# A planner that reckons a longer landing for small adding loads, with the output's and gate's steps placed anew

## The chip, the cores and the metric

One core of one Trainium2 chip runs the whole program once per launch. The metric is the device time of one execution in microseconds (us). The time of the kernel before is the median of three runs, 981.69 us (978.53 to 984.54).

## The reference: what is computed

One layer of a decoder trunk is applied to 1024 prompt positions and to 8 sample positions (one new position of each of 8 sequences), with a model width of 1024. All data are fp32.

```python
xn = rmsnorm(x, pre_g)
u, v, z_a, x_b, z_b, g_a, g_b = split(xn @ w_in)          # seven parts of 1024 columns
y_a = gelu(u) * (tril(w_s) layernorm(gelu(v)) + b_s) * silu(z_a)   # mixed inside chunks of 128
y_b = pooled_linear(x_b) * silu(z_b)                      # trailing windows of 2, 4, 8, 16
m = sigmoid(g_a) * (y_a @ w_pa) + sigmoid(g_b) * (y_b @ w_pb)
h = x + rmsnorm(m @ w_out, post_g)
y = h + rmsnorm(sigmoid(rmsnorm(h, ple_in_g) @ w_pg) * (p @ w_ple), ple_out_g)
```

The outputs are y of the prompt and of the sample, and small states (normalised v rows, pooling rows).

## The kernel before, in words

**Products.** Each large product is cut into 2x2 quarters and done in seven block products instead of eight (functions strassen and strassen_within), and each fp32 factor is split into a high and a low float32r part, so that one block product is 12 matmuls (k = 4 slices, three terms) of 512 columns, or 24 of 260. The blocks have the names of their right-hand factor: B11, T2, T3, T1, B21, B22, T4. In the last two stages the tokens stand on the left: the stage of the output (m @ w_out; tiles acct, left factors mw, right factors woB and woT) and the stage of the gate (h @ w_pg; left factors hw, right factors wgB and wgT). Each has four pairs of token tiles (pair 0 to 3, of 2 x 128 tokens), seven block products a pair. The lists oflow and gflow hold these 28 + 28 steps in order: steps 0 to 27 are the output's, 28 to 55 the gate's. Three PSUM tiles named acct go round; a product that opens a tile waits until the tile's last reader has let go of it.

**Sample rows.** The 8 sample rows go beside these, without the seven-block scheme: sample_steps loads two rows tiles of 128 x 1024 of the weight (worow, wgrow) at one step and runs 8 matmuls of 8 x 512 (tile sps) two steps later, four times. OS and GS (line 36) are the steps at which this begins in the two stages. After the last of them, out_sample adds the partial rows up (sodd, hs).

**From the output to the gate.** For each token tile and for the sample, out_finish scales the row by its norm, adds x with an adding load issued by GpSimd (`nc.gpsimd.dma_start(out=h, in_=x_of(t), accum_op=ALU.add)`) and stores h; gate_norm takes the sum of squares of the finished h on ScalarE (junk<-h, for the sample hn<-hs) and its root on GpSimd; gate_input loads h back in 32-row blocks (hblocks, four DMAs) which VectorE turns (STREAM_TRANSPOSE) into the tile big. For the sample the turning is done by TensorE (tile psst). TURNS (line 35) has for each pair the steps after which its out_finish, gate_norm and gate_input are recorded; for the sample they are the steps OS + 10, OS + 12 and OS + 15 of oflow.

**The planner.** All of this is recorded first (all instructions bear line 369, the line that plays them). Planner.take, lines 213 to 245, gives each operation a reckoned length; a DMA gets `moved` (MB, doubled for an adding load) and `lands`, the time to land on top of its bytes. Planner.wanted goes back from the clock of TensorE's recorded order and sets when each operation is due (`late`), and Planner.order then plays all five engines forward: an operation may start no sooner than its due time less a lead (LEAD, or LOAD for a load into a fresh slot), the one due soonest goes first, and slots are handed out. The order in which each engine's instructions stand, and the slot of each tile, come from this. On the chip no reckoned time is left: an instruction runs as soon as those ahead of it in its engine's queue are through and what it waits for is done. SyncE (SP) issues nearly all DMAs in one queue, where a DMA that waits for its slot holds up all behind it.

Of the kernel before, what the change touches and what calls it, by code (L numbers as in the profile page):

```python
# [31 lines left out]
PUSH = {'norm': -5.0, 'half': 0.0, 'cut': 0.0, 'e': -4.0, 'we': -4.0, 'vw': -5.0, 'p': -1.0}  # L32
WARM = 8
HASTE = 8.0
TURNS = ((7, 8, 11), (14, 14, 18), (21, 26, 28), (30, 33, 35))
OS, GS = 5, 12
WINDOWS = (2, 4, 8, 16)
PLE = 256
SLOTS = 46
# [55 lines left out]
class Planner:  # L95
# [5 lines left out]

    SEEN = {"tensor": 0.25, "vector": 0.15, "scalar": 0.20, "gpsimd": 0.20}
    TABLES = {AF.Gelu_apprx_tanh: 1, AF.Sigmoid: 2, AF.Silu: 3}
    LOAD, LEAD, PATIENCE, RATE, SPARE = 14.98, 14.0, 55.8, 0.36, 3
    SPARED = 1.0

    def __init__(self, nc, slots, queues):
# [98 lines left out]
    def take(self, engine, method, args, kwargs):  # L206
        given = [*(("out" if i == 0 else "", a) for i, a in enumerate(args)), *kwargs.items()]
        writes = [a for k, a in given if k in ("out", "accum_out") and a is not None]
        reads = [a for k, a in given if k not in ("out", "accum_out") and hasattr(a, "tensor")]
        if kwargs.get("accum_op") is not None:  # L210
            reads += writes
        name = writes[0].tensor.name
        if engine == "tensor" and self.open is not None and self.open[0] == name:
            op = self.open[1]
        else:
            op = Op(engine, len(self.ops), self.clock, self.fixed)
            op.patience, op.push = self.patience, self.push
            self.ops.append(op)
        self.open = (name, op) if engine == "tensor" else None
        op.calls.append((method, args, kwargs))  # L220
        op.spent.append(op.busy)
        if method == "dma_start":
            run = min(self.run(a) for a in (writes[0], reads[0]))
            op.busy, op.moved = 1.0 if engine == "gpsimd" else 0.45, writes[0].size() * 4e-6 * (1 + 0.2 / run)
            op.lands = 2.0
            if kwargs.get("accum_op") is not None:
                op.moved, op.lands = 2 * op.moved, 3.5
        else:
            took = self.duration(engine, method, writes[0], reads, kwargs)
            op.busy += took  # L230
            if engine == "tensor" and not self.fixed:
                self.clock += took
            if engine == "scalar":
                op.table = self.TABLES.get(kwargs["func"], 0)
        for ap in reads:
            self.touch(op, ap, False)
        for ap in writes:
            self.touch(op, ap, True)
# [133 lines left out]
@with_exitstack  # L372
def tile_hybrid_step(ctx, tc, *args):
    hybrid_step(ctx, tc, *args)


def hybrid_step(
# [116 lines left out]
    class Operand:  # L494
# [37 lines left out]
        def at(self, what, k):  # L532
            return [part[:, k % 2, :] for part in self.parts[what, k // 2]]
# [653 lines left out]
    def stored(key, src, width, free=None):  # L1187
        return Stored(key, src, kept[key + "low"], kept[key + "high"], width, free)
# [194 lines left out]
    flat, c = big.rearrange("p b t -> p (b t)"), [T + 4 * w for w in (0, HALF, HALF + WIDE, HALF + 2 * WIDE)]  # L1383
# [20 lines left out]
    c = vsteps[0]  # L1404
# [55 lines left out]
    WITHIN = ("B11", "T2", "T3", "T1", "B21", "B22", "T4")  # L1460

    def turn_over(op, loads, cuts, parts=PARTS):
        for what, l, c in zip(parts, loads, cuts):
            at(l, lambda what=what: op.load(what))
            at(c, lambda what=what: op.cut(what))

    p, l, c = gbsteps[2], gbsteps[3], pasteps[0]
    turn_over(yaop, l, [*l[1:], c[0]])
    p, l, c = pasteps[2], pasteps[3], pbsteps[0]
# [97 lines left out]
    def hasty(do, ts):  # L1567
        plan.patience = HASTE
        for t in ts:
            do(t)  # L1570
        plan.patience = plan.PATIENCE
# [61 lines left out]
    def embed_gate_sample(ps):  # L1633
# [3 lines left out]
        for j in range(2):  # L1637
# [7 lines left out]
    woop, wgop = stored("wo", w_out, HALF), stored("wg", kept["wg"], HALF)  # L1645
    outsteps = [strassen_within(Turned(i, "m"), woop, Out(i)) if i else
                strassen(Turned(i, "m"), woop, Out(i), Tokens, FIRST) for i in range(NPAIR)]
# [8 lines left out]
    l, c = pbsteps[3], outsteps[0]  # L1656
    turn_over(woop, l, [*l[2:], c[0], c[1]], ("B11", "T3", "T2", "B21", "T4", "T1", "B22"))
    l, c = outsteps[3], gatesteps[0]
    turn_over(wgop, [*outsteps[2][4:], *l], [*l[2:], c[0], c[1]], WITHIN)

    def gain_row(key, src):
        gains[key] = row_broadcast(src, key)
# [11 lines left out]
    for i in range(NPAIR):  # L1674
        ts = [2 * i + 1, 2 * i]
        for do, s in zip((out_finish, gate_norm, gate_input), TURNS[i]):
            at((oflow + gflow)[s], lambda do=do, ts=ts: hasty(do, ts))
# [198 lines left out]
```

## Time and profile before

| | before |
|---|---|
| median of three runs | 981.69 us (978.53 to 984.54) |
| profiled execution, own time | 979.92 us |
| its span, first to last instruction | 978.2 us |
| TensorE (PE) busy | 965.4 us, 99% |
| VectorE (DVE) busy | 805.7 us, 82% |
| ScalarE (ACT) busy | 495.5 us, 51% |
| GpSimd (POOL) busy | 72.8 us, 7% |
| mean granted TensorE clock | 0.997 |

In the profile, PE is the row of matmuls, PEld that of weight loads, DVE, ACT and POOL are the three other compute engines, SPq the DMA issues of SyncE. A row of the timeline has the start and length in us, the engine, the line, the operation, the tile written and the tiles read, shapes, the count, and in brackets how long the engine sat idle before it and what ended that. Matmuls overlap, so each is shown longer (0.39 us) than the 0.23 us from one start to the next.

### The profile page before, as it was taken

How to read it: one execution, taken by the hardware profiler on the slowest of the kernel's cores; microseconds unless marked ns; L12 is line 12 of the kernel's file. 1: busy time of each engine (PE TensorE's matmuls, PEld its weight loads, DVE VectorE, ACT ScalarE, POOL GpSimd, SP SyncE). 2: the span in 40 equal slices, each digit the busy share in tenths (PEclk: the TensorE clock that was granted, in tenths of full speed). 3: DMA queues.
4: the chain of work that ended last, by engine and by line, in shares of the span. 5: the costliest groups of instructions: out<-in, count | busy, mean ns of one | idle time of the engine just before them, and what ended most of it. 6: DMA issues, size and time to landing. Idle time of an engine off the chain costs nothing. (4 is left out here: it accounts for less than half of the span.)

```text
span 978.2 us, 15914 instructions
## 1 busy us (share of the span) xinstructions
PE 965.4 (99%) x6048; PEld 858.1 (88%) x6048; DVE 805.7 (82%) x1251; ACT 495.5 (51%) x847; POOL 72.8 (7%) x117
## 2 busy tenths in 40 slices
PE   9999999999999999999999999999999999999996
PEld 7889999999999998999999999999999997778775
DVE  7798568978879789887777897698699899779987
ACT  7674346767434544242423343463363273688655
POOL 2200000000000000000010100000000001323212
PEclk9999999999999999999999999999999999999998
DMA  9464654423457787541222266692592385698996
GB/s 347 148 151 88 152 135 148 162 95 116 171 213 275 257 281 238 188 153 54 87 76 93 75 218 244 222 376 91 170 370 87 120 306 177 160 300 296 222 326 209
DMA packets 128505, 185.81 MB, mean 190 GB/s; under 512 B 42150, under 2 KB 85198, under 8 KB 128421
## 3 DMA queue, kind: packets, MB, share of 16 engines
q1 hardware_dynamic: 126093, 176.91, 54.4%
q0 software_dynamic: 2048, 7.37, 4.2%
q8 instruction: 47, 0.77, 0.3%
q10 hardware_dynamic: 288, 0.52, 0.2%
q14 instruction: 29, 0.24, 0.1%
HBM read 129.27 MB, written 55.96 MB: 189 GB/s over the span
## 5 line engine op out<-in xcount | busy, mean ns | idle before, releaser
L369 DVE TENSOR_TENSOR u<-acc,u 128x520 f32<-128x520 f32 (+1 forms) x90 | 62.5, 695 | 29.8 <-PE acc L369 29.8
L369 POOL TENSOR_TENSOR rstd<-ms,mhalf 128x1 f32<-128x1 f32 (+1 forms) x37 | 30.1, 840 | 448.7 <-DVE ms L369 448.0
L369 ACT ACTIVATE u<-acc 128x512 f32<-128x512 f32 x39 | 23.2, 596 | 35.0 <-PE acc L369 32.5
L369 ACT ACTIVATE zbw<-zbs 128x512 fp32r<-128x512 f32 x16 | 10.0, 629 | 31.6 <-DVE zbs L369 25.8
L369 DVE TENSOR_TENSOR big<-big 128x1024 f32<-128x1024 f32 (+4 forms) x20 | 24.7, 1262 | 0.1
L369 POOL COPY big<-xb 128x1 f32<-128x1 f32 x8 | 3.5, 443 | 260.9 <-ACT xb L369 218.0
L369 ACT ACTIVATE big<-mix 128x256 f32<-128x256 f32 x32 | 11.9, 382 | 20.6 <-PE mix L369 19.7
L369 ACT ACTIVATE paw<-pas 128x512 fp32r<-128x512 f32 x16 | 10.1, 630 | 24.0 <-DVE pas L369 20.0
L369 ACT ACTIVATE pbw<-pbs 128x512 fp32r<-128x512 f32 x16 | 10.1, 630 | 22.3 <-DVE pbs L369 17.0
L369 PE MATMUL accm<-qh,wpoolw 128*128 128x260 f32 (+1 forms) x96 | 21.0, 320 | 0.0
L369 DVE TENSOR_TENSOR zbw<-zbs,zbw 128x512 fp32r<-128x512 f32 x16 | 10.9, 689 | 12.0 <-ACT zbw L369 11.9
L369 ACT ACTIVATE gbw<-gbs 128x512 fp32r<-128x512 f32 x16 | 10.1, 630 | 20.9 <-DVE gbs L369 11.7
L369 ACT ACT_TABLE_LOAD x11 | 14.1, 1283 | 7.4 <-PE acc L369 3.6
L369 ACT ACTIVATE junk<-h 128x512 bf16<-128x512 f32 x25 | 15.7, 627 | 3.5 <-DVE h L369 3.0
L369 DVE SCALAR_TENSOR_TENSOR zb<-accm,gvec,zb 128x512 f32<-128x512 f32 (+1 forms) x16 | 12.0, 750 | 6.5 <-PE accm L369 6.4
L369 PEld LDWEIGHTS accm<-qh,wpoolw 128*128 128x128 f32 x96 | 15.6, 189 | 1.9
L369 ACT ACTIVATE u<-acct 128x512 f32<-128x512 f32 x22 | 13.0, 590 | 7.4 <-PE acct L369 5.1
L369 DVE TENSOR_TENSOR paw<-pas,paw 128x512 fp32r<-128x512 f32 x16 | 10.9, 687 | 6.7 <-ACT paw L369 6.7
L369 ACT ACTIVATE mw<-ms 128x512 fp32r<-128x512 f32 x16 | 10.0, 625 | 12.4 <-DVE ms L369 9.7
L369 ACT ACTIVATE xbw<-xbs 128x512 fp32r<-128x512 f32 x16 | 10.0, 626 | 11.7 <-DVE xbs L369 10.0
L369 PE MATMUL mix<-wst,vh 128*128 128x256 f32 x64 | 15.6, 321 | 0.0
L369 ACT ACTIVATE uw<-us 128x512 fp32r<-128x512 f32 x16 | 10.0, 625 | 10.0 <-DVE us L369 5.9
(660 smaller groups left out, 3557.7 us busy)
## 6 DMA issues: line engine op xcount, KB each, us to landing
ga<-ga SPq DMA_DIRECT2D x16, 516.0 KB, 5.9
gb<-gb SPq DMA_DIRECT2D x16, 516.0 KB, 7.2
ya<-za SPq DMA_DIRECT2D x8, 516.0 KB, 4.9
yb<-zb SPq DMA_DIRECT2D x8, 516.0 KB, 2.6
x<-in_x_prompt_dram SPq DMA_DIRECT2D x8, 512.0 KB, 7.3
vraw<-in_w_in_dram SPq DMA_DIRECT2D x8, 512.0 KB, 5.9
e<-e SPq DMA_DIRECT2D x8, 512.0 KB, 5.9
vturned<-v SPq DMA_DIRECT2D x32, 128.0 KB, 3.4
```

Of the source, the lines that this page charges most:

```text
L369: getattr(getattr(self.nc, e), method)(*(self.real(a) for a in args), **{k: self.real(a) for k, a in kwargs.items()})
```

## The change

Five things are changed. Two are rules of the planner: the lead of loads into fresh slots goes from 14.98 to 13.919 us, and an adding load that moves no more than 0.3 MB is reckoned to land in 7.0 us instead of 3.5. A full adding load of 128 x 1024 has a `moved` of 1.1 MB and keeps 3.5, so this touches one load alone, the sample's of 8 x 1024 in out_finish. Three move recorded steps: OS from 5 to 7 (the sample's loads, sums, norm and turning in the output's stage, two steps later); TURNS of pair 1 (gate_norm after step 15 instead of 14) and of pair 3 (out_finish after step 28 instead of 30); and the loads of the gate's right-hand blocks (the list wgop), whose seven parts begin at the sixth step of the output's pair 2 instead of the fifth.

```diff
-TURNS = ((7, 8, 11), (14, 14, 18), (21, 26, 28), (30, 33, 35))
-OS, GS = 5, 12
+TURNS = ((7, 8, 11), (14, 15, 18), (21, 26, 28), (28, 33, 35))
+OS, GS = 7, 12
...
-    LOAD, LEAD, PATIENCE, RATE, SPARE = 14.98, 14.0, 55.8, 0.36, 3
+    LOAD, LEAD, PATIENCE, RATE, SPARE = 13.919, 14.0, 55.8, 0.36, 3
...
             if kwargs.get("accum_op") is not None:
-                op.moved, op.lands = 2 * op.moved, 3.5
+                op.moved, op.lands = 2 * op.moved, 3.5 if op.moved > 0.3 else 7.0
...
     l, c = outsteps[3], gatesteps[0]
-    turn_over(wgop, [*outsteps[2][4:], *l], [*l[2:], c[0], c[1]], WITHIN)
+    turn_over(wgop, [*outsteps[2][5:], *l], [*l[2:], c[0], c[1]], WITHIN)
```

The instructions are the same in kind and number on every engine. TensorE's order is the same up to the middle of the output's stage; the other queues differ by small exchanges from the first stage on. Three places follow.

First ScalarE, in the output's stage, where the sample's sum of squares stands (hn is the sample's normed row, hs its row, acct the PSUM tiles of the block products, h a token tile). Before:

```order
L369 ACTIVATE junk,ssq_531<-h_8964 128x512
L369 ACTIVATE hn_9166,ssq_539<-hs_9047 8x1024
L369 ACTIVATE junk,ssq_538<-h_9130 128x512
L369 ACTIVATE junk,ssq_542<-acct_521 128x512
L369 ACTIVATE h_9190<-acct_521 128x512
L369 ACTIVATE hn_9166<-hs_9047,rstd_541 8x4x8x32
L369 ACTIVATE junk,ssq_543<-acct_534 128x512
L369 ACTIVATE h_9190<-acct_534 128x512
```

and in the change:

```order
L369 ACTIVATE junk,ssq_536<-h_9131 128x512
L369 ACTIVATE junk,ssq_539<-acct_518 128x512
L369 ACTIVATE h_9186<-acct_518 128x512
L369 ACTIVATE junk,ssq_540<-acct_523 128x512
L369 ACTIVATE h_9186<-acct_523 128x512
L369 ACTIVATE mw_9205<-big 128x512
L369 ACTIVATE mw_9212<-ms_9108 128x512
L369 ACTIVATE hn_9218,ssq_542<-hs_9084 8x1024
L369 ACTIVATE mw_9228<-big 128x512
L369 ACTIVATE u_9237<-acct_547 128x512
L369 ACTIVATE hn_9218<-hs_9084,rstd_544 8x4x8x32
```

The sample's two steps stood ahead of the two copies that empty acct tiles of pair 2; now they stand behind both.

Second SyncE, in the middle of the gate's stage: hblocks are the rows of h to be turned (4 DMAs a token tile), wgrow the weight rows of the sample's matmuls. Before:

```order
L369 DMA h<-h_9343 128x1024
L369 DMA hblocks_9644<-h 32x4x256 x4
L369 DMA wgrow_9663<-wg 128x1024
L369 DMA wgrow_9670<-wg 128x1024
L369 DMA h<-h_9365 128x1024
L369 DMA hblocks_9684<-h 32x4x256 x4
L369 DMA wgrow_9706<-wg 128x1024
L369 DMA wgrow_9719<-wg 128x1024
L369 DMA out_dram<-ge_9538 128x1024
L369 DMA hblocks_9798<-h 32x4x256 x4
```

and in the change:

```order
L369 DMA hblocks_9588<-h 32x4x256 x4
L369 DMA h<-h_9347 128x1024
L369 DMA wgrow_9654<-wg 128x1024
L369 DMA wgrow_9660<-wg 128x1024
L369 DMA h<-h_9367 128x1024
L369 DMA wgrow_9693<-wg 128x1024
L369 DMA wgrow_9701<-wg 128x1024
L369 DMA hblocks_9782<-h 32x4x256 x4
L369 DMA out_dram<-ge_9525 128x1024
L369 DMA hblocks_9812<-h 32x4x256 x4
```

The last hblocks of pair 2 now stand ahead of the store of h, and the first of pair 3 behind the second couple of wgrow. By the slots, the first of pair 3 now waits for the last matmul of block product T4 of the gate's pair 1.

Third TensorE, at the start of the gate's stage; each shown row is the first of a block product, and what stands between is the rest of it. Before:

```order
L369 MATMUL acct_571<-wgT3h_9315,hw_9394 128x512
...
L369 MATMUL acct_570<-wgT1h_9340,hw_9349 128x512
...
L369 MATMUL acct_569<-wgB21h_9399,hw_9420 128x512
...
L369 MATMUL acct_570<-wgB22h_9481,hw_9497 128x512
...
L369 MATMUL acct_571<-wgT4h_9502,hw_9424 128x512
...
L369 MATMUL acct_594<-wgB11h_9265,hw_9443 128x512
```

and in the change:

```order
L369 MATMUL acct_575<-wgT3h_9314,hw_9392 128x512
...
L369 MATMUL acct_569<-wgB21h_9405,hw_9423 128x512
...
L369 MATMUL acct_574<-wgT1h_9344,hw_9399 128x512
...
L369 MATMUL acct_594<-wgB11h_9263,hw_9441 128x512
...
L369 MATMUL acct_574<-wgB22h_9483,hw_9501 128x512
...
L369 MATMUL acct_575<-wgT4h_9505,hw_9428 128x512
```

B21 of pair 0 goes ahead of T1, and B11 of pair 1 ahead of B22 and T4 of pair 0; pairs 1 and 2 are exchanged in the same way.

## The prediction

> **What bounds the kernel now.** I read the page's first part, then busy times by stretch, then TensorE's waits, and only then the timeline where the longest wait in mid-program stands. First the page, and the stretches (each engine's busy us, and its instructions in brackets, then the granted clock and the DMA engines' share):
>
> ```profile
> span 978.2 us, 15914 instructions
> PE 965.4 (99%) x6048; PEld 858.1 (88%) x6048; DVE 805.7 (82%) x1251; ACT 495.5 (51%) x847; POOL 72.8 (7%) x117
> ```
>
> ```profile
> 820.00:886.00 66.00, 64.82 (x297) 48.62 (x296) 53.37 (x91) 48.59 (x100) 16.21 (x19) 1.00 0.80 220
> 886.00:950.00 64.00, 64.00 (x289) 48.10 (x289) 56.62 (x92) 41.93 (x83) 19.48 (x16) 1.00 0.93 272
> ```
>
> PE is busy for 99% of the span. The change's steps lie in the second and third stretch, the output's stage and the gate's. In the third PE has no gap, in the second 66.00 - 64.82 = 1.18 us. All of PE's waits that the trace names:
>
> ```profile
> PE warm L369 <- DVE heat L369: 1.5, 1, 1.5
> PE acct L369 <- ACT h L369: 1.2, 1, 1.2
> PE acc L369 <- DVE za L369: 0.7, 1, 0.7
> PE acct L369 <- ACT ge L369: 0.6, 1, 0.6
> PE e L369 <- DVE pl L369: 0.2, 1, 0.2
> ```
>
> Together 4.2 us, 0.4% of the span. Since no matmul is taken out, an order of instructions can gain no more than these and a little of the tail behind the last matmul: faster by over 1% (9.8 us, about what a measurement of this kernel can tell from no change) is nearly shut out. For slower nothing shuts it out, since every new wait of PE is paid in full.
>
> The 1.18 us is one wait. On PE (matmuls of the sample's tile sps, of acct, and the sample's turning psst):
>
> ```profile
> 843.87 1.04 PE L369 MATMUL sps<-worow,big 128*8 128x512 f32 x8
> ...
> 864.17 0.39 PE L369 MATMUL acct<-woT4h,mw 128*128 128x512 f32 x1
> ...
> 865.74 0.50 PE L369 MATMUL acct<-woB11h,mw 128*128 128x512 f32 x1 [1.18 <-ACT h L369]
> ...
> 868.72 0.66 PE L369 MATMUL psst<-ident,hn 8*128 8x8 f32 x8
> ...
> 874.96 0.39 PE L369 MATMUL acct<-woT1h,mw 128*128 128x512 f32 x1
> ```
>
> The first matmul of B11 of the last pair could have begun at 865.74 - 1.18 = 864.56; its acct tile was let go only by ACT's h<-acct. ACT in that stretch, then who held ACT up:
>
> ```profile
> 856.42 0.63 ACT L369 ACTIVATE mw<-ms 128x512 fp32r<-128x512 f32 x1 [4.30 <-DVE ms L369]
> ...
> 857.96 0.62 ACT L369 ACTIVATE junk<-h 128x512 bf16<-128x512 f32 x1
> ...
> 858.70 0.63 ACT L369 ACTIVATE junk<-h 128x512 bf16<-128x512 f32 x1
> ...
> 862.67 1.06 ACT L369 ACTIVATE hn<-hs 8x1024 f32<-8x1024 f32 x1 [1.73 <-DMA hs<-in_x_sample_dram]
> ...
> 863.72 0.61 ACT L369 ACTIVATE junk<-h 128x512 bf16<-128x512 f32 x1
> ...
> 864.51 0.60 ACT L369 ACTIVATE junk<-acct 128x512 bf16<-128x512 f32 x1
> ...
> 865.10 0.59 ACT L369 ACTIVATE h<-acct 128x512 f32<-128x512 f32 x1
> ...
> 865.57 1.14 ACT L369 ACTIVATE hn<-hs,rstd 8x1024 f32<-8x1024 f32 x1
> ```
>
> ```profile
> 856.34 0.85 POOL L369 DMA_DIRECT2D hs<-in_x_sample_dram  x1 [1.86 <-DVE hs L369]
> ```
>
> ```profile
> 857.70 0.68 DVE L369 TENSOR_TENSOR h<-acct,u 128x512 f32<-128x512 f32 x1
> ```
>
> POOL issued the sample's adding load at 856.34 and ACT could go on at 862.67, 6.3 us later, where the planner before reckoned 3.5. The sample's sum of squares waited 1.73 us, and the two steps that empty pair 2's acct tile stood behind it. So the late thing is the load; ACT has time (48.59 of 66 us busy), only its order is in the way.
>
> **The change part by part.** It removes nothing and adds nothing; all prices are waits.
>
> *The 7.0 us and OS = 7.* They put hn behind both readers of acct, as front's first pair of orders shows. Then ACT goes on from 857.96 with five sums over h, one each 858.70 - 857.96 = 0.74 us: the fifth ends at 857.96 + 5 x 0.74 = 861.7. The h that this fifth reads (863.72 before) came from DVE at 857.70 + 0.68 = 858.4, so it needn't wait. junk<-acct then takes till h<-acct's start, 865.10 - 864.51 = 0.6, to 862.3, and h<-acct its 0.59: acct is free near 862.9, where PE wants it at 864.56. That leaves 1.6 us of slack in place of 1.18 of wait. Term: **-1.2 us**. Between its bounds 0 (something else holds the tile) and -1.2 I take the full value, since 1.6 us of slack outlasts one more ACT step of the dearest kind here (1.14).
>
> What moves with the sample: two steps are two block products. T2 and T3 run from psst's end, 868.72 + 0.66 = 869.4, to T1's start at 874.96, two in 5.6 us, so the last sps ends at 844.91 + 5.6 = 850.5 rather than 844.91 (843.87 + 1.04). Its copies from sps on ACT, some 3 us with the rest of out_sample, then fall near 851 to 856, where ACT sat idle for 4.30 us; I cost them at nothing, and at most at their 3 us less the 1.6 of slack, 1.4, if that idle time closes. The next thing that could be late is psst, which turns the sample's hn and now stands two blocks later, ahead of T1: 874.96 - 1.18 - 0.66 (psst's own time, no longer ahead) = 873.1. From the last sps to the load's landing went 862.67 - 844.91 = 17.8 us, and from there to the end of the second hn 865.57 + 1.14 - 862.67 = 4.0. Taken the same way from 850.5: 868.3 and 872.3, 0.8 us ahead of psst. Cost 0, the end of slack near.
>
> By the Trainium skill, page "DMA: Bandwidth & Descriptors", section "Anatomy of one DMA — SWDGE (gpsimd) path", a transfer issued from GpSimd has a fixed cost near 2 us and then runs at about 436 GB/s; 32 KB would by that rule be through in about 2.1 us, an estimate. It speaks against the 7.0: the old 3.5 would have been enough, ACT's 1.73 us wait would be none of the load's, and this term would be 0. The trace differs: the load took 6.3 us, with the DMA engines 80% busy in that stretch.
>
> *LOAD 13.919.* Loads into fresh slots may start 14.98 - 13.919 = 1.06 us later than before. What that touches is seen first where a load is already short:
>
> ```profile
> 375.18 0.69 DVE L369 TENSOR_TENSOR xbs<-xbraw,xbraw 128x512 f32<-128x512 f32 x1 [1.89 <-DMA xbraw<-in_w_in_dram]
> ```
>
> ```profile
> 379.06 0.51 PE L369 MATMUL acc<-xB22h,zaw 128*128 128x260 f32 x2 [0.75 <-DVE za L369]
> ```
>
> DVE waits 1.89 us for xbraw, za is queued behind, and PE pays 0.75. SyncE's queue around this load stands in the same order, behind the same waits, so I expect the 0.75 to stay: term 0, bounds -0.75 (gone) and +1.06 (the whole lead at that load).
>
> *TURNS and wgop.* In the gate's stage the steps come in another order at a few places; each engine does the same work, PE had no gap there in 64.00 us, but DVE was busy for 56.62 of them and has 7.4 to spare. The dearest move is that of pair 3's hblocks, priced below; from the bounds 0 and +2.0 I take 0. The last wait (0.6 <-ACT ge) is in the tail and none of these steps is ahead of it: 0, at best -0.6.
>
> **Sum.** -1.2 + 0 + 0 + 0 = -1.2 on the profiled execution: 979.92 - 1.2 = 978.7 (span 977.0). That execution is 981.69 - 979.92 = 1.8 us below the median of runs, so the median goes to 981.69 - 1.2 = **980.5**.
>
> **Rivals.** *A, a new wait in the gate's stage (slower).* For it:
>
> ```profile
> 916.56 3.04 SPq L369 DMA_DIRECT2D hblocks<-h  x4
> ...
> 929.51 2.11 SPq L369 DMA_DIRECT2D hblocks<-h  x4
> ```
>
> ```profile
> hblocks<-h SPq DMA_DIRECT2D x4, 128.0 KB, 10.1
> ```
>
> ```profile
> hblocks<-h SPq DMA_DIRECT2D x4, 128.0 KB, 6.7
> ```
>
> ```profile
> 928.10 0.97 PE sps L369 x8
> ...
> 948.25 0.97 PE sps L369 x8
> ```
>
> ```profile
> 929.88 1.24 DVE L369 STREAM_TRANSPOSE big<-hblocks 128x1024 f32<-128x1024 f32 x1
> ...
> 931.62 0.68 DVE L369 TENSOR_TENSOR hs<-big,hs 128x512 f32<-128x512 f32 x1
> ...
> 936.32 2.48 DVE L369 SCALAR_TENSOR_TENSOR ge<-ge,rstd,out 128x1024 f32<-128x1024 f32 x2 [0.46 <-POOL rstd L369]
> ```
>
> ```profile
> 945.32 0.40 PE L369 MATMUL acct<-wgT4h,hw 128*128 128x512 f32 x1
> ```
>
> The first hblocks of pair 3, issued before at 916.56, now wait for T4 of the gate's pair 1, whose end is the start of sps at 928.10, less 1.2: 926.9. Issuing takes 2.1; landing 6.7 (the row of the stretch 928 to 938) or 10.1 (that of 915 to 928): 935.7 or 939.1. DVE has these rows first in a train of two turnings (1.24 each), two of ge by rstd (2.48 / 2 each), two sums (0.68) and one that empties acct (0.68): 2 x 1.24 + 2 x 1.24 + 3 x 0.68 = 7.0, so 942.7 or 946.1. T4 of pair 2 wants that acct at 945.32 - 1.2 = 944.1: no wait with 1.4 to spare, or 2.0 of wait. A decides from a landing of 8.1 us on. Against it: the 93% DMA share that made 10.1 has that same hblocks in it, and the move spreads them. With 2.0: 980.5 + 2.0 = 982.5.
>
> *B, the wait is only replaced.* PE no longer waits at 864, but at psst, as 0.8 us of slack hangs on a landing of 6.3. Another row of POOL's adding loads has more:
>
> ```profile
> h<-in_x_prompt_dram POOLq DMA_DIRECT2D x3, 512.0 KB, 8.2
> ```
>
> With 8.2 psst waits 8.2 - 6.3 - 0.8 = 1.1, and what is saved is given back but for 0.1; B decides from a landing of 7.1 on. Or the wait at 864 was not the load's, and nothing is gained. Either gives 981.6 to 981.7; I say 981.7.
>
> *C, the shorter lead bites in the body.* Of each seventh of w_in there are eight loads:
>
> ```profile
> vraw<-in_w_in_dram SPq DMA_DIRECT2D x8, 512.0 KB, 5.9
> ```
>
> 7 x 8 = 56 loads, at 1.06 each and no slack anywhere, are 59 us. But PE's list of waits has one such place in the whole program, so nearly all have more slack than that. Over 1% slower takes (9.8 + 1.2) / 1.06, some 10 loads that all lie bare: 980.5 + 10 x 1.06 = 991.1.
>
> **How the numbers follow.** The forecast has 0.60, as the 1.6 us of slack behind its one term outlasts any single step of ACT there. A has 0.20, as one of two landings decides it; B 0.15, of which 0.03 are that the load isn't the cause, as by the rule on GpSimd's transfers; C 0.05. The single runs reach 3.2 below and 2.9 above their median; for a median of three I take some 2 either way. Low: 980.5 - 0.75 - 0.6 - 2.2 = 977.0; high: A and the 1.06 at xbraw, 983.5, and 2.0: 985.5. By the bound of 1%, faster 0.02 (runs' spread alone), slower 0.04 (most of C, and A's upper end), within 0.94.
>
> **What would show it.** Right: no PE wait acct <- ACT h near 864; ACT's hn<-hs behind h<-acct, with or without a wait of its own; psst near 873 without a bracket; the 0.75 of za still there; PE without gap from 886 to 950; the span near 977.0. Wrong: a bracket on psst (B), on T4 of the gate's pair 2 with DVE waiting for hblocks near 936 to 939 (A), or new waits of PE for DVE before 820 with a load behind them (C).

## The result and the profile after

| | before | changed |
|---|---|---|
| median of six runs | 981.32 us (978.53 to 984.54) | 990.62 us (987.55 to 995.60) |
| profiled execution, own time | 979.92 us | 990.48 us |
| its span | 978.2 us | 988.8 us |
| PE's named waits | 4.2 us | 10.3 us |

The change is slower: ratio 1.0099, 95% interval 1.0079 to 1.0120. The forecast was 980.5 in a range of 977.0 to 985.5.

The page of the changed kernel, and the same two stretches as before:

```profile
span 988.8 us, 15915 instructions
...
PE 970.2 (98%) x6048; PEld 860.0 (87%) x6048; DVE 805.5 (81%) x1251; ACT 500.6 (51%) x847; POOL 67.4 (7%) x117
```

```profile
820.00:886.00 66.00, 64.21 (x294) 47.87 (x292) 51.21 (x90) 42.99 (x88) 16.71 (x19) 1.00 0.78 224
886.00:950.00 64.00, 63.00 (x277) 48.74 (x276) 60.10 (x96) 46.59 (x92) 13.53 (x16) 1.00 0.94 273
```

The stretch from 820 to 886 has an idle 1.79 us in place of 1.18, and the stretch that had no gap now has 1.0. Over the whole program DVE and ACT are busy about as long as before (805.5 and 500.6 us). PE's waits:

```profile
PE acct L369 <- ACT u L369: 3.8, 2, 2.1
PE acc L369 <- DVE za L369: 1.7, 1, 1.7
PE acct L369 <- ACT ge L369: 1.6, 2, 1.0
PE warm L369 <- DVE heat L369: 1.5, 1, 1.5
PE pp L369 <- DMA p<-in_p_prompt_dram: 1.1, 1, 1.1
PE e L369 <- ACT wehi L369: 0.6, 1, 0.6
```

The wait acct <- ACT h, which the forecast was about, is gone; so is the 0.75 us near 379, which it expected to stay. Two of the list, 1.1 (pp) and 0.6 us (e), lie in the first 9 us, where every queue still stands in the order of before; they come from that execution. Four others stand in the middle and at the end of the program:

```profile
342.35 0.51 PE L369 MATMUL acc<-xB22h,zaw 128*128 128x260 f32 x2 [1.74 <-DVE za L369]
...
880.46 0.51 PE L369 MATMUL acct<-woT1h,mw 128*128 128x512 f32 x1 [1.70 <-ACT u L369]
...
906.96 0.50 PE L369 MATMUL acct<-wgB11h,hw 128*128 128x512 f32 x1 [1.00 <-ACT ge L369]
...
966.96 0.50 PE L369 MATMUL acct<-wgT1h,hw 128*128 128x512 f32 x1 [2.08 <-ACT u L369]
```

And behind two of them the granted clock (the column ahead of the last two) falls to half for 3.4 us, which no wait shows, since PE counts as busy:

```profile
342.30:346.50 4.20, 4.15 (x21) 4.15 (x22) 4.13 (x6) 2.17 (x4) 0.00 (x0) 0.59 0.48 192
...
967.00:971.50 4.50, 4.50 (x13) 3.54 (x14) 4.39 (x7) 2.44 (x5) 1.74 (x2) 0.62 0.17 22
```

4.2 x 0.41 and 4.5 x 0.38 are 1.7 us each. Behind the old 1.18 us wait, from 866 to 870, the clock was 1.00. The sum over the two profiled spans: waits 10.3 - 4.2 = 6.1, half clock 3.4, together 9.5 of 10.6 us; the rest has no row of its own.

**Where three of the waits come from.** Near 340 the two loads of uraw are issued late. SyncE before, then in the change (PE stood 1.8 us later than before by then, 1.3 of them from the first 10 us):

```profile
318.93 0.39 SPq L369 DMA_DIRECT2D uraw<-in_w_in_dram  x1
...
321.80 0.38 SPq L369 DMA_DIRECT2D uraw<-in_w_in_dram  x1
```

```profile
302.13 0.32 SPq L369 DMA_DIRECT2D wolow<-woraw  x1
302.86 0.32 SPq L369 DMA_DIRECT2D wohigh<-woraw  x1
303.28 1.77 SPq L369 DMA_DIRECT2D zaraw<-in_w_in_dram  x2
...
321.66 0.32 SPq L369 DMA_DIRECT2D ya<-za  x1
...
323.30 0.45 SPq L369 DMA_DIRECT2D uraw<-in_w_in_dram  x1
...
326.45 1.62 SPq L369 DMA_DIRECT2D uraw<-in_w_in_dram  x1
```

```profile
336.18 0.69 DVE L369 TENSOR_TENSOR us<-uraw,uraw 128x512 f32<-128x512 f32 x1 [4.69 <-DMA uraw<-in_w_in_dram]
```

The lead was cut by 1.06 us; uraw is issued 4.4 and 4.7 us later, 2.6 and 2.9 beside PE. VectorE, with the step that empties PE's acc into za behind uraw, sits 4.69 us. Ahead of uraw stands a store of ya, issued at 321.66 as soon as its data were done. The last step that makes them is a small addition on VectorE, before and in the change:

```profile
315.01 0.15 DVE L369 TENSOR_TENSOR za<-za,smixs 128x8 f32<-128x8 f32 x1
```

```profile
321.48 0.16 DVE L369 TENSOR_TENSOR za<-za,smixs 128x8 f32<-128x8 f32 x1
```

Before, one other step stands between it and the step that it adds to (313.27); in the change thirteen do (from 310.57 on). That this holds uraw up is read from the rows; no run moved this step alone.

Near 880 it is VectorE's order together with a late load. The second turning of pair 2's hblocks waits for its load, and the sum into acct stands behind it; then ScalarE's u<-acct, then PE. The turning stood ahead of the sum before, too (869.89 and 872.45), but there its rows had landed. In the change:

```profile
877.94 1.25 DVE L369 STREAM_TRANSPOSE big<-hblocks 128x1024 f32<-128x1024 f32 x1 [2.82 <-DMA hblocks<-h]
879.11 0.67 DVE L369 TENSOR_TENSOR acct<-acct,u 128x512 f32<-128x512 f32 x1
```

Near 966 VectorE waits for eback (rows of e, which the gate is multiplied with). Its issues, and VectorE:

```profile
943.37 16.92 SPq L369 DMA_DIRECT2D eback<-e  x5
```

```profile
958.24 0.69 DVE L369 TENSOR_TENSOR ge<-eback,ge 128x512 f32<-128x512 f32 x1 [3.81 <-DMA eback<-e]
958.85 0.68 DVE L369 TENSOR_TENSOR ge<-acct,u 128x512 f32<-128x512 f32 x1
```

```profile
959.02 0.63 ACT L369 ACTIVATE junk<-ge 128x512 bf16<-128x512 f32 x1 [3.93 <-DVE ge L369]
```

Beside PE this load is not late. Its first issue stands 15.8 us ahead of the last pair's first matmul of T2 in the change (943.37 and 959.15) and 15.1 before (936.95 and 952.04), where the five stand in one row as well. But VectorE comes to the step that reads it 4.7 us ahead of that matmul (958.24 - 3.81 = 954.43), and before only 2.4 (949.64): the step now stands ahead of a ge<-acct, behind which it stood. ScalarE waits with it, and u<-acct, for which PE waits at 966.96, comes late on ScalarE.

### The profile page after: what moved, and what is told of

Read it like the earlier page. It is cut to its first block, busy times and chain, and to the rows that moved or that the text cites. A ratio compares the mean times of both kernels' runs of the same rounds, so it can differ in the third digit from the quotient of the medians.

```text
span 988.8 us, 15915 instructions
## 1 busy us (share of the span) xinstructions
PE 970.2 (98%) x6048; PEld 860.0 (87%) x6048; DVE 805.5 (81%) x1251; ACT 500.6 (51%) x847; POOL 67.4 (7%) x117
## 5 line engine op out<-in xcount | busy, mean ns | idle before, releaser
L369 DVE TENSOR_TENSOR ge<-eback,ge 128x512 f32<-128x512 f32 (+2 forms) x19 | 12.4, 659 | 5.2 <-DMA eback<-e 3.8
L369 ACT ACTIVATE gaw<-gas 128x512 fp32r<-128x512 f32 x16 | 10.0, 627 | 12.1 <-DVE gas L369 8.4
L369 PE MATMUL mix<-wst,vh 128*128 128x256 f32 x64 | 15.5, 320 | 0.0
L369 ACT ACTIVATE gbw<-gbraw 128x512 fp32r<-128x512 f32 x12 | 7.5, 628 | 15.6 <-DMA gbraw<-in_w_in_dram 10.4
```

The lines of the kernel that those rows point to most:

```text
L369: getattr(getattr(self.nc, e), method)(*(self.real(a) for a in args), **{k: self.real(a) for k, a in kwargs.items()})
```

## The experiments

Each ratio is to runs of the kernel before that were made beside that run; their medians are 980.5 to 981.5 us. In brackets stands its 95% interval.

**One rule alone, and the change without it.** First the kernel before with only the lead changed:

```diff
-    LOAD, LEAD, PATIENCE, RATE, SPARE = 14.98, 14.0, 55.8, 0.36, 3
+    LOAD, LEAD, PATIENCE, RATE, SPARE = 13.919, 14.0, 55.8, 0.36, 3
```

> The kernel before with the lead of loads at 13.919 and nothing else changed. Theory: the shorter lead by itself makes the load of uraw late near 340 us, PE waits about 1.7 us for DVE's za there and then runs some 3.4 us at half clock (1.6 us more), while the old 0.75 us wait at 379 goes. So +2.6 in the first 800 us, PE waits acc<-DVE za 1.7 near 340, and a total of 983.5 to 985 if the last stages stay as before. Rival: the late uraw comes from the other edits (the planner goes back from the end), and the lead alone gives 981 to 982 with no such wait near 340.

Measured 990.02 us, ratio 1.0095 (1.0069 to 1.0121): from this one number nearly as much as the whole change loses, and far more than expected. The wait near 340 is there (1.00 us in the profiled execution, with no half clock behind it). Most of the rest was lost in the last stages: PE waits of 2.0 us in all for ACT u and 1.6 for DVE hw, and a longer tail: behind the last matmul 12.7 us pass (974.8 to 987.5) where before there were 8.5 (969.7 to 978.2). One piece of that tail is a root on GpSimd, in the chain of waits of this run:

```profile
979.00 2.27 POOL rstd L369
```

Then the change with that line put back, all else kept:

> The change with the lead put back to 14.98, all else as in the change. Theory: the first 800 us are as before (0.75 us wait near 379, no wait near 340), and the last stages cost what they cost in the change: 1.2 us gained at 865, and 1.7, 1.0 and 2.1 us of wait plus 1.5 us of half clock lost behind it: 985.5 to 988.5. Rival: the last stages lose only because the lead also moved their loads; then the whole is at or below the time of before, 980 to 981.5.

Measured 982.69, ratio 1.0020 (1.0001 to 1.0039). This is nearer to the rival, though 1.2 us above its range: without the lead the other four edits together cost 0.2%. Its waits in the last two stages:

```profile
PE acct L369 <- ACT ge L369: 1.6, 2, 1.1
...
PE acct L369 <- ACT u L369: 1.0, 1, 1.0
```

The gain near 865 is there, and a wait of 1.0 us at T1 of the last pair and 1.1 near 900 give it back.

**Longer and half as short.** The kernel before with LOAD at 15.5 and at 14.45:

> The kernel before with the lead of loads longer, 15.5 instead of 14.98, nothing else. Theory: shorter leads are what hurts (loads come later), so a longer one costs nothing: 980 to 981.5 with no new wait. Rival: any redrawing of the last stages costs several us, whichever way the number is turned, since the order before is a picked one: 984 or more, with new PE waits behind 820 us and none before.

> The kernel before with the lead of loads at 14.45, half of the way to the change's 13.919. In SyncE's queue the two stores already stand ahead of zaraw as in the change. Theory: the wait near 340 is there with 1 to 1.7 us (a step in the order, not something that grows with the lead), and the total is 984 to 990. Rival: what is lost is in proportion to the lead, about half of 9 us: 985, spread over many small waits of loads.

Measured 983.17, ratio 1.0021 (1.0007 to 1.0035), and 986.44, ratio 1.0062 (1.0042 to 1.0082). So a longer lead, which redraws the orders too, costs 0.2%. That is above the theory's 981.5 and below the rival's 984: any redrawing costs something so far, but not several us. With shorter leads it goes 0, 0.6% and 0.95% for 14.98, 14.45 and 13.919. At 14.45 the wait near 340 was 1.0 us and the others behind the start under 0.75 each: both expectations of that run fit its time, and it does not tell them apart.

**The lead in the body or at the end.** In the change, with `o.late` the planner's due time (the second kernel has `>=`):

```diff
-                lead = self.LOAD if o.moved and o.fresh else self.LEAD
+                lead = (14.98 if o.late < 800.0 else self.LOAD) if o.moved and o.fresh else self.LEAD
```

> The change, but loads that are due before 800 us (by the planner's reckoning) keep the lead of 14.98; only those of the last two stages have 13.919. Theory one: the shorter lead hurts where it applies, in the body by the late uraw (2 to 3.7 us with the half clock) and in the last stages by late hblocks and eback; here the body's part is gone: 985 to 988. Theory two: the short lead in the last stages costs nothing by itself, and what the change loses there comes from slots and an order that the body hands on: about the time without the shorter lead, 981.5 to 983.5.

> The change, but only loads due before 800 us have the lead of 13.919; those of the last two stages have 14.98. Theory one: the late uraw near 340 remains, 2 to 3.7 us, and the last stages are as without the shorter lead: 984 to 986.5. Theory two: the last stages lose as much as in the change, since what is handed on from the body decides: 988 to 991.

Measured 986.66, ratio 1.0054 (1.0035 to 1.0073), and 986.71, ratio 1.0050 (1.0032 to 1.0069). Theory one's times hold, the second but for 0.2 us: over the 0.20% of the kernel without the lead, the lead at the end adds 0.34% and in the body 0.30%, 3.3 and 2.9 us; with the 2.0 us of the rest that is 8.2 of the change's 9.7 us. Each interval is some 0.2% wide to either side, so by an estimate from them such a sum is sure to 3 us only.

Where each kernel loses is told by PE's lag behind the kernel before. PE's matmuls stand in the same order until 823 us, so the start of the same matmul can be compared, and at the end the last one's and the span (profiled executions, us):

| kernel | in the first 10 us | to 822 us | to the last matmul | behind it |
|---|---|---|---|---|
| the change | 1.3 | 3.7 | 6.0 | -0.5 |
| without the lead | 0.1 | -1.0 | 1.4 | 0.1 |
| short lead at the end | 3.3 | -1.1 | 4.5 | 0.1 |
| short lead in the body | 0.3 | 1.6 | 1.7 | -0.1 |
| lead alone | 0.1 | 2.0 | 2.9 | 4.3 |

The first column is not the edits' doing, since all queues still stand in the order of before there. In the body the kernels with the short lead there lose 2.6 to 4.7 us more than the two without it; in the last stages the two of the change's kernels with the short lead there lose 3 to 5 us more than the two without it. That is theory one by its places. In the body not all of it is seen at uraw: in the run with the short lead there, the wait near 340 was 0.7 us, another near 380 was 0.6, and the rest has no row. The -1.0 says that the 0.75 us near 379 was missing with the lead of 14.98 too.

At the end, the traces say, the lead acts through VectorE's order. In both kernels the first eback is issued as long ahead of the last pair's T2 (940.46 and 956.25 with the short lead at the end, 939.72 and 955.42 without). With it VectorE comes to eback 4.7 us ahead of T2 and waits, as in the change, and PE behind it; without it the step stands behind a ge<-acct, 2.3 us ahead of T2, and nothing waits. With the short lead at the end, then without:

```profile
954.85 0.69 DVE L369 TENSOR_TENSOR ge<-eback,ge 128x512 f32<-128x512 f32 x1 [3.29 <-DMA eback<-e]
```

```profile
963.58 0.51 PE L369 MATMUL acct<-wgT1h,hw 128*128 128x512 f32 x1 [1.61 <-ACT u L369]
```

```profile
951.76 0.69 DVE L369 TENSOR_TENSOR ge<-acct,u 128x512 f32<-128x512 f32 x1 [0.39 <-PE acct L369]
...
953.10 1.29 DVE L369 TENSOR_TENSOR ge<-eback,ge 128x512 f32<-128x512 f32 x2
```

**The small load's 7.0 and OS alone.** The kernel before with these two lines of the change:

> The kernel before with the small adding load reckoned at 7.0 and OS at 7, nothing else. Theory of the prediction: these two alone take away PE's 1.2 us wait for acct near 865 and nothing comes in its place: 980.0 to 980.6. Rival: the sample's steps, two later, hold a slot that pair 2's adding load waits for (in the change that load waited 3.29 us for ACT's sodd), so hblocks of pair 2 come late and PE waits 1.7 us at T1 of the last pair near 875: 981.5 to 983.

Measured 988.23, ratio 1.0067 (1.0044 to 1.0089): slower by more than either expected, and the wait is at another place, psst:

```profile
PE psst L369 <- ACT hn L369: 3.8, 1, 3.8
```

```profile
874.45 3.62 POOL L369 TENSOR_TENSOR rstd<-ms,mhalf 8x1 f32<-8x1 f32 x1
```

```profile
878.11 1.15 ACT L369 ACTIVATE hn<-hs,rstd 8x1024 f32<-8x1024 f32 x1 [2.40 <-POOL rstd L369]
```

Here the sample's chain is later still (hn is summed at 872.50), and its root on GpSimd, right behind two of GpSimd's adding loads (872.94), shows 3.62 us. Behind PE's wait the clock was half for 6.8 us (878.80 to 885.60), and the tail behind the last matmul is 11.1 us long instead of 8.5. So rival B of the prediction exists, in this combination of the edits; in the full change psst has no bracket. The losses of the edits don't add up: these two and the lead lose 0.67% and 0.95% alone, and all five together 0.99%.

**Two stores behind the loads.** The change, with SyncE's order edited at one place (rows of that queue):

```diff
-wolow<-woraw
-wohigh<-woraw
 zaraw<-in_w_in_dram
 zaraw<-in_w_in_dram
+wolow<-woraw
+wohigh<-woraw
```

> The change with two DMAs put elsewhere in SyncE's queue: the stores of wolow and wohigh that stand ahead of the two zaraw loads of the seventh and eighth column block (issued 302.1 and 302.9 after SyncE sat still from 291) go behind those loads. Nothing else is moved. Theory: these stores hold the loads up, zaraw lands some 4 us later than before, all on VectorE behind it is late, the store of ya waits for it and holds uraw up in turn; with the loads ahead of the stores PE's 1.7 us wait for za near 340 goes and so does the half clock behind it, 3.4 to 3.7 us in all: 986.5 to 987.5. Rival: uraw is late for another reason (the queue is full anyway): the wait stays and the time is 990 to 991.

Measured 989.76, ratio 1.0093 (1.0053 to 1.0133), not to be told from the change. zaraw is now issued at 299.22, as early as before (299.11), and uraw still at 321.62 and 324.88. So the two stores are not what makes uraw late; the store of ya (319.99) still stands ahead of it, just behind VectorE's small addition (319.80). The wait near 340 was 1.4 us in the profiled execution, without half clock behind it, and T1 of the last pair waited 3.9 us. In the next run, with the same body, the wait near 340 was under 0.2: how long PE waits behind a late uraw hangs on when it lands in that execution.

**The turning behind the sum.** To the same kernel, on VectorE:

```diff
-STREAM_TRANSPOSE big<-hblocks
 acct<-acct,u
+STREAM_TRANSPOSE big<-hblocks
```

> As the run with the two stores behind zaraw, and on VectorE the second turning of pair 2's hblocks (which waited 2.82 us for its load at 877.94) goes behind the sum into acct that stood behind it. Theory: PE's 1.7 us wait at T1 of the last pair near 880 comes from this order alone; it falls under 0.5 us and the time falls by 1.2 to 1.7 us against the run with the stores moved alone: 985 to 986. Rival: the turning is then late for PE itself, and the wait shows again on the next products (acct <- DVE hw or ACT hw near 885 to 890), time as without it.

Measured 986.78, ratio 1.0053 (1.0025 to 1.0081), 3.0 us under the run before it, though the two intervals overlap. T1 follows psst without a wait, though the turning still waits for its load:

```profile
871.31 0.70 DVE L388 TENSOR_TENSOR acct<-acct,u 128x512 f32<-128x512 f32 x1 [1.35 <-PE acct L388]
873.09 1.25 DVE L388 STREAM_TRANSPOSE big<-hblocks 128x1024 f32<-128x1024 f32 x1 [1.08 <-DMA hblocks<-h]
```

So the wait at T1 comes from this order when hblocks are late: it was 1.7 us in the change and 3.9 in the run before this one, by waits of VectorE for hblocks of 2.82 and 4.75. What moving the turning is worth is less sure: near 901 a wait of 1.5 us stands at the gate's next product (1.0 in the change), which the run before did not have.

**The forecast's term by itself.** The kernel before, with only the sample's sum of squares (and its mean and root) moved:

```diff
-hn<-hs (sum of squares)
 junk<-h
 junk<-acct
 h<-acct
+hn<-hs (sum of squares)
```

> The kernel before, with one thing moved and nothing drawn anew: the sample's sum of squares on ScalarE, with the mean on VectorE and the root on GpSimd that hang on it, goes behind the two steps that empty pair 2's first acct tile. Theory: this is the term of -1.2 us of the prediction by itself: PE's wait for acct <- ACT h near 865 goes, psst stays free of waits, and the time is 1.2 us under the kernel before, ratio 0.9988, about 980.0 to 980.5. Rival: the wait goes to psst (3.8 us in the run with the small load's 7.0 and OS alone), ratio over 1.000.

Measured 979.07, ratio 0.9982 (0.9966 to 0.9997), a gain of 0.3 to 3.3 us: faster than both kernels. On ScalarE the sum of squares still waits for its load, and nothing of pair 2 is behind it:

```profile
862.98 0.59 ACT L385 ACTIVATE h<-acct 128x512 f32<-128x512 f32 x1
864.15 1.06 ACT L385 ACTIVATE hn<-hs 8x1024 f32<-8x1024 f32 x1 [0.58 <-DMA hs<-in_x_sample_dram]
```

PE's first matmul of B11 starts at 864.86 with no wait. This profiled execution had a wait of 1.7 us at T1, by the same turning (it waited 1.51 us for its load), although VectorE's and SyncE's queues stand as in the kernel before. So a wait at T1 can come without any edit of the change. The next kernel was to take it out. There the turning stands behind the sum, and the copy of wgB on ScalarE that takes over hblocks' slot behind the turning:

> The kernel before with the sample's sum of squares behind the emptying of acct (as in the run with that alone) and, on VectorE, the second turning of pair 2's hblocks put behind the sum into acct for which PE's T1 of the last pair waits; a copy of wgB on ScalarE that takes hblocks' slot goes behind the turning with it. Theory: the wait at T1 (1.7 us in one execution of the run before this) hangs on when hblocks land, as in the change; with the turning behind, it is gone in every execution: 978 to 979.5, ratio 0.997 to 0.998. Rival: the turned rows are then late for the gate's first products near 885 to 895 (PE waits for hw), ratio 0.999 or more.

Measured 981.52, ratio 0.9997 (0.9984 to 1.0010): no gain. The copy then waited for the turning, and u<-acct stood behind the copy, so that T1 still waited 1.3 us:

```profile
876.29 1.06 ACT L392 ACTIVATE wgB11h<-wgB 128x1024 fp32r<-128x1024 f32 x1 [1.68 <-DVE big L392]
877.25 0.61 ACT L392 ACTIVATE hw<-big 128x512 fp32r<-128x512 f32 x1
877.77 0.58 ACT L392 ACTIVATE u<-acct 128x512 f32<-128x512 f32 x1
```

Neither the theory nor its rival had that: the queue behind the wait had moved to another engine. The best version measured is the one with the single move.

**The half clock.** Two kernels without the layer, trains of matmuls with pauses, each run once:

> No part of the layer is computed: trains of 40 to 47 matmuls of 128x512 with a pause between, in which VectorE copies 384 to 3072 columns, eight times each; outputs are filled with what is there. Theory: a pause of PE over about 1.7 us (half of a stretch of 3.4 us) can halve the granted clock for about 3.4 us behind it, some 1.6 us of loss, and pauses under 1.3 us never do; between, it depends on how the pause lies. Rival: the clock falls only after pauses of 3.4 us or more, and the half clock seen at 343 and 968 us of the change has another cause.

> As the run of trains of matmuls with pauses (no part of the layer is computed; outputs are filled with what is there), with nine lengths of pause from about 1.5 to 2.3 us, sixteen times each. Theory: the clock is halved when a pause fills more than half of one of the stretches of 3.4 us that the clock's control counts, wherever these begin; so pauses up to 1.7 us never halve it in full trains, the share rises from there, and above 2 us nearly all do. Rival: a sharp limit near 1.9 us, below which none and above which all are followed by half clock.

By the bracket that the profile gives each pause, and counting the pauses that are followed by eight or nine matmuls at 0.43 us instead of 0.23:

| pause, us | up to 1.65 | 1.72 | 1.79 | 1.85 | 1.99 | 2.12 |
|---|---|---|---|---|---|---|
| first run | none of 87 | | | 6 of 8 | | |
| second run | none of 63 | none of 16 | 3 of 16 | 9 of 16 | 8 of 16 | 7 of 16 |

Each costs 1.7 us, in 3.4 us. So the first run's theory holds and its rival, pauses of 3.4 us or more, falls. There is a limit below which it never came in full trains, near 1.75 us, and above it about half of the pauses up to 2.1 us are followed by half clock.

Which half, the trace's record of the clock tells. The spells of half clock start on a fixed grid: the first five of the second run start at 1043.50, 1104.94, 1132.25, 1231.24 and 1255.13, which are 18, 8, 29 and 7 times 3.413 us apart, and all 27 fit so. The two of the change (343.08 and 967.72) are 183 times 3.413 apart. Of the 72 pauses of 1.79 us and more in both runs, 33 lie whole between two points of that grid, and 30 of these are followed by half clock, from the next point on. The other 39 are cut by a point, and only 3 are followed; these have 1.98 us or more on one side. So the theory of the second run had the mechanism, stretches of 3.4 us wherever they begin, with a limit of some 1.8 us within one stretch instead of 1.7; its share above 2 us was wrong, since a pause of 2.1 is often cut.

The waits of the change fit: 1.74 and 2.08 lie whole in a stretch and were followed, 1.00 was not, and of the 1.70 at T1 only 1.49 lie in one stretch. So do the two long ones, 3.8 and 3.9 us in other runs, with 3.3 and 3.4 in one stretch, both followed. One wait of mid-program did not fit the limit: in the run with the short lead in the body, 1.31 us at T1 was followed by half clock. (In the first 10 us, where the clock has only just come up, 4.9 to 6.8 us from the start, waits of 1.39 and of 0.93 and 0.83 us were followed in two runs, and 1.12 and 0.57 in the change were not.) Ahead of that wait at T1 stand psst's eight small matmuls, 0.66 us in which PE does little:

```profile
874.73 0.66 PE L369 MATMUL psst<-ident,hn 8*128 8x8 f32 x8
876.70 0.74 PE L369 MATMUL acct<-woT1h,mw 128*128 128x512 f32 x1 [1.31 <-ACT u L369]
```

```profile
876.50:880.00 3.50, 3.30 (x8) 2.62 (x9) 3.50 (x4) 3.50 (x6) 2.14 (x2) 0.54 1.05 387
```

The two together are 1.97 us, and lie in one stretch. That small matmuls count as a pause is read from this one case, not shown by a run of its own.

By the Trainium skill, page "TensorE: Matmul & The Clock Gate", section "Part 1: The HAM clock gate (the "warmup" mystery)", the clock falls to half after a stretch of about 3.4 us without work, counted in stretches that run on whatever the kernel does. The length of the half clock here agrees with that figure (3.4 us), and so does the fixed grid; the pause that sets it off does not, since 1.74 us was enough in the change and 1.79 in the trains.

## Why the prediction was wrong, step by step

- **What bounds the kernel, and that no order could gain over 0.4%:** right. So was "every new wait of PE is paid in full", which is even too little: some bring 1.7 us of half clock on top. That the change's steps lie in the second and third stretch was not: the lead redraws the queues from 63 us on.
- **The term of -1.2 us (sample's sum behind the emptying of acct):** right as a move of that sum, shown by itself at 0.9982 (0.9966 to 0.9997), with the wait gone and 1.3 us between the end of h<-acct (863.57) and PE's B11 (864.86), where 1.6 were reckoned. In the change the wait at 865 is gone too. But the term was written for the planner's two lines, the 7.0 and OS, and these alone measured 988.23: with them the planner moves more than that sum; "Cost 0" for psst was a wait of 3.8 us there. By the figure of the Trainium skill, page "DMA: Bandwidth & Descriptors", section "Anatomy of one DMA — SWDGE (gpsimd) path", that the prediction weighed, this term would have been 0; the run does not bear that out, and its load took 7.2 us.
- **LOAD 13.919, "term 0, bounds -0.75 (gone) and +1.06 (the whole lead at that load)":** this step failed. Alone it measured 990.02, +9.5 us by the medians of that set. Put back, with all else of the change kept, it leaves 982.69, inside the forecast's 977.0 to 985.5. Three things were wrong in the step. It looked only at the place that waited already (379), and not at where the orders change. That wait went away, but by luck: it is missing in four other profiled runs with the lead of 14.98 in the body, and stands at 0.4 to 0.8 us in four with 13.919. It took the lead as the most that a load can be late; but the planner redraws every engine's queue from it, and a late step is late by what stands ahead of it: uraw 2.6 and 2.9 us beside PE, behind a store that waits for a step of VectorE which ran 9.7 us after the one that it adds to; and at eback no load is late beside PE, but VectorE asks for it 2.3 us earlier. And it counted a wait at its own length, without the half clock.
- **Rival C** had the right cause and sign at a chance of 0.05. Its price, "some 10 loads that all lie bare", was made from equal shares of 1.06 us; the loss came at a few places, 3.7 us in the body and 6.0 in the last stages of the profiled execution.
- **TURNS and wgop at 0:** open in part. T1 of the last pair (1.0 us without the lead, 1.7 in the change) and the gate's first products (1.1 and 1.0) wait where the page of before has no wait; without the lead they cost about what the term of -1.2 gives. No run has TURNS or wgop alone, and the wait at T1 came in a run with the old ones too (1.7 us, the single move). In sign this is like rivals A and B, at places that neither named: A's T4 has no wait, B's psst only in the run with two of the edits.
- **Against rival C stood** "SyncE's queue around this load stands in the same order": true of xbraw near 379, and no evidence for the rest of SyncE's queue.

What stays open: that the short lead loses time in the body and in the last stages is shown by runs; the single steps on VectorE that do it are read from traces, and of them only the turning ahead of the sum was moved by a run. Why the lead alone, without the other edits, loses 4 us behind the last matmul was read from one chain only. Every kernel whose orders the planner drew anew is slower than before, by 0.2% at the least, also with the longer lead, so part of the loss may be that of leaving a picked order, whichever way; no run separates this. The 0.95% of the lead alone and the 0.99% of the change are not the sum of parts in each place: the places differ from kernel to kernel.

## What to carry to other kernels

Where a planner's number redraws a queue, don't price the edit by its own size: look with the orders of both kernels for every load that now stands behind a store or a wait, and for every step that waits for a load and now stands ahead of one that the bounding engine needs, and price the whole time until that is through. A kernel whose bounding engine is at 99% has all its slack in other queues; a wait that is lifted there by moving one instruction can be worth its length, if the move puts nothing else behind a wait, and the same wait lifted by a global rule is paid for at places that the profile of before cannot show. Count a wait of PE of some 1.8 to 2.1 us as 1.7 us longer in half of the cases; which half hangs on where the stretches of 3.4 us begin in that execution.

## What was not expected of the hardware

The half clock behind pauses of 1.75 us is the main one, with its fixed grid of 3.413 us. GpSimd's root of 8 x 1 took 0.54 us in one place and 3.62 in another, the long one right behind two of its adding loads; but the loads are not what makes it long in general, since the same step on 128 x 1 took this in the kernel before, 18 us after the last adding load:

```profile
894.16 7.27 POOL L369 TENSOR_TENSOR hscales<-ms,mhalf 128x1 f32<-128x1 f32 x1 [0.82 <-DVE ms L369]
```

Why is open. The sample's adding load of 32 KB, 6.3 us from issue to landing before, took 4.7 in the change, 3.5 with the short lead in the body and 7.2 with the single move, so neither 3.5 nor 7.0 is its length. And the same program's waits vary from one execution to the next: two kernels with the same body waited 1.4 and under 0.2 us near 340, and the kernel before and that with the single move, with the same body too, 0.75 us and not at all near 379.
